# One inference step of a hybrid convolution / RWKV-7 decoder: block inversions as a stream of their own, and the last layer's MLP once per token group

## The chip, the cores and the metric

The kernel runs on one core of one Trainium2 chip. The metric is device time in microseconds (us) for one execution of the whole step; smaller is better. Three runs of the kernel before are shown, and one further execution was profiled.

## What is computed

The reference is a two-layer trunk over 1040 prompt tokens (16 learned meta tokens and 1024 prompt tokens) and 8 sampled tokens, model width 1024. Layer 0 mixes tokens with a Conformer convolution, layer 1 with RWKV-7; both are followed by a squared-ReLU MLP of width 4096. Cut to what matters here:

```python
def _wkv7_step(S, inp):
    r_t, w_t, k_t, v_t, kk_t, a_t = inp
    sa = jnp.einsum('bhvk,bhk->bhv', S, -kk_t)
    S = (S * w_t[:, :, None, :] + sa[..., None] * (kk_t * a_t)[:, :, None, :]
         + v_t[..., None] * k_t[:, :, None, :])
    y = jnp.einsum('bhvk,bhk->bhv', S, r_t)
    return S, y

def _sqrelu_mlp(h, w_in, w_out):
    return jnp.square(jax.nn.relu(h @ w_in)) @ w_out
...
    for i in range(DEPTH):
        ...
        h = h + out
        h = h + _sqrelu_mlp(_rmsnorm(h, norm_mlp[i]), w_mlp_in[i], w_mlp_out[i])
    return (_rmsnorm(h, norm_final), ...)
```

## The kernel before

**Arithmetic.** Everything is float32. A large product is made of three matmuls in a reduced-precision format: each operand is split into a high and a low part, and hi·hi, lo·hi and hi·lo are added in PSUM (`mm3`, lines 211 to 213). A weight tile of 128x1024 is loaded by SyncE (SP), its high part is made by ScalarE (ACT, line 177, `_hi`), and its low part by GpSimd (POOL) in four pieces, or by VectorE (DVE) in one (line 182, `_lo`). Raw tiles and split tiles go around in rings of a few buffers.

**Layer 0.** Convolution, then the MLP in three passes over the token groups `G0` of about 350 columns. In a pass, all 32 column tiles of `w_mlp_in` and 32 tiles of `w_mlp_out` are loaded and split once. Two passes have other work written beside them (the next group's convolution, above all DVE work). The third runs beside the first RWKV mixer group.

**Layer 1, mixers.** `mixer_in(g)` runs for four groups `G1` of 256 to 272 tokens: the projections k, r and v of eight tiles each (matmuls named `p_k`, `p_r`, `p_v`), low-rank parts, decays, and the operands of the recurrence, which go to DRAM. At the end of each tile, `finish` writes the 32x32 blocks `d_n` that are to be inverted.

**The recurrence** is done in 17 chunks: chunk 0 has the 16 meta tokens, chunks 1 to 16 have 64 tokens each. `front(c)` loads a chunk's operands and makes the products `A`; `chunk(c)` makes `gg`, `bT`, `W`, `po`, `U`, `S` and the output `Y` (lines 1284, 1311, 1351, 1359), each a short burst of small matmuls that waits for DVE or ACT to have moved the burst before. The state `sv` passes from chunk to chunk. Between chunks, `inverses(c, n)` inverts the blocks of chunk 0, and then of four chunks at a time (1 to 4, 5 to 8, ...), as 30 column steps of two DVE operations (lines 1243 and 1244), in SBUF. It is called inside `front(c)` for c = 0, 1, 5, 9 and 13, so it is part of the recurrence's one stream of work.

**What sets the order.** Each engine executes its own list in order. The lists come from the program's order and a scheduler's choice among what is ready. In the program, side work is a generator that gets `next()` at fixed places of the main work: `tick` gives the recurrence credit at each place of mixers 1 to 3 (`PACE`), and `filler(points, ...)` spreads several streams over the points of an MLP pass (`FA`, `NGA`, `NGB`, `FB` are the lengths it assumes).

**Layer 1, output and MLP.** Token groups `G2` have 328, 352 and 352 columns. After the mixers, `norm_gate` makes the gated output `z` of 128 tokens at a time from finished chunks, and `mixer_out(g)` multiplies by `rwkv_w_o` (`ps_oo`) and adds to the residual `h1`. Group 0 then has an MLP pass of its own, with the rest of the recurrence, the decode step of the 8 sampled tokens (`decode_step`, `ddec`, `Sdec`) and the gates of groups 1 and 2 beside it. Groups 1 and 2 have `mixer_out` one after the other, and then one common MLP pass in which each weight tile is used for both groups; `final(g)` (last norm, transposes `pf`, store) of groups 0 and 1 lie beside it.

**Buffers.** `new_act` makes an activation's high and low part as one tile each over all 8 row blocks (`[P, KT, n]`). `z` and the MLP's input `m1` of a group share one buffer.

## Time and profile before

| | us |
|---|---|
| median of 3 runs | 2793.69 |
| lowest and highest of them | 2791.5, 2795.14 |
| the profiled execution's own time | 2785.31 |
| its span from first to last instruction | 2783.6 |

| engine | busy us | share of the span |
|---|---|---|
| PE (matmul) | 2606.4 | 94% |
| DVE | 1994.5 | 72% |
| POOL | 1645.4 | 59% |
| ACT | 1355.2 | 49% |

The shares are averages over unlike stages, so they say little by themselves; the stages are cut apart in the rows below. TensorE's granted clock has two levels here, 2.4 GHz (1.0) and 1.2 GHz (0.5); the mean over the span was 0.973. A stretch with less than 1.0 ran in part at the lower level. DMA moved 428.32 MB, 154 GB/s on average.

### The profile page before, as it was taken

To read this page: it belongs to the slowest core of one execution; us is meant where nothing else is said; L and a number is where in the kernel's file an instruction comes from. 1 tells how busy PE (TensorE), PEld (TensorE's weight loads), DVE (VectorE), ACT (ScalarE), POOL (GpSimd) and SP (SyncE) were. 2 spreads that over 40 slices of the span, in tenths; PEclk is the share of its full clock that TensorE was granted. 3 is DMA by queue.
4 is the path that set the end of the run, shared out by engine and by line. 5 is a ranking of instruction groups with operands and counts; after the bars stand their busy time and mean duration, and the time that the engine had idled before them with its cause. 6 is when DMAs were issued, how large, how long until landed. Compare 5 with 4: busy or idle time off the path is not lost.

```text
span 2783.6 us, 54198 instructions
## 1 busy us (share of the span) xinstructions
PE 2606.4 (94%) x20554; PEld 2517.6 (90%) x20554; DVE 1994.5 (72%) x3752; ACT 1355.2 (49%) x2520; POOL 1645.4 (59%) x2191
## 2 busy tenths in 40 slices
PE   7998999999998999988789799979999999999998
PEld 7998999999998999978688688868889999999998
DVE  5999999996457454787897886877897654434445
ACT  5545444543355444565567757745434552222223
POOL 6686877887786354645443546647568773333332
PEclk9999999999999999998899899989999999999999
DMA  6563544454444555677788878876666632222211
GB/s 182 165 191 92 157 137 137 135 178 136 139 136 144 153 155 169 198 202 193 206 211 212 239 177 208 232 195 176 162 186 198 180 114 88 69 69 69 69 54 42
DMA packets 659284, 428.32 MB, mean 154 GB/s; under 512 B 126841, under 2 KB 609209, under 8 KB 659023
## 3 DMA queue, kind: packets, MB, share of 16 engines
q1 hardware_dynamic: 652780, 421.93, 54.0%
q8 instruction: 162, 2.65, 0.4%
q10 hardware_dynamic: 6018, 2.89, 0.4%
q14 instruction: 100, 0.81, 0.1%
q0 software_dynamic: 224, 0.03, 0.0%
HBM read 353.03 MB, written 72.66 MB: 153 GB/s over the span
## 4 chain that ended last, share of the span: by engine, by line
PE 59%; DVE 17%; POOL 8%; DMA 7%; issue 5%; ACT 4%; SPq 0%; DVEq 0%; ACTq 0%; POOLq 0%
PE ps_in L213 7%; PE ps_in L212 7%; PE ps_in L211 7%; PE out L212 7%; PE out L211 7%; PE out L213 7%; POOL wo_lo L182 4%; POOL wi_lo L182 3%; DVE cv L553 1%; DVE ni L1244 1%; DVE tt L1243 1%; DVE h L383 1%; PE ps_g L211 1%; PE ps_g L213 1%; PE ps_g L212 1%
## 5 line engine op out<-in xcount | busy, mean ns | idle before, releaser
L182 POOL TENSOR_TENSOR wo_lo<-wo_raw,wo_hi 128x256 fp32r<-128x256 f32 x672 | 521.8, 810 | 316.6 <-ACT wo_hi L177 294.2
L182 POOL TENSOR_TENSOR wi_lo<-wi_raw,wi_hi 128x256 fp32r<-128x256 f32 x600 | 464.7, 808 | 294.3 <-ACT wi_hi L177 284.4
L211 PE MATMUL out<-hh,wo_hi 128*128 128x352 f32 (+2 forms) x1536 | 498.9, 327 | 22.7 <-DVE h L383 10.5
L211 PE MATMUL ps_in<-m_h,wi_hi 128*128 128x352 f32 (+2 forms) x1536 | 498.0, 324 | 7.9 <-ACT m_h L304 6.2
L383 DVE TENSOR_TENSOR h<-h,out 128x352 f32<-128x352 f32 (+2 forms) x768 | 382.4, 508 | 167.3 <-PE out L213 166.6
L212 PE MATMUL out<-hh,wo_lo 128*128 128x352 f32 (+2 forms) x1536 | 496.2, 323 | 2.2 <-DVE wo_lo L182 2.2
L213 PE MATMUL ps_in<-m_l,wi_hi 128*128 128x352 f32 (+2 forms) x1536 | 495.1, 323 | 0.5 <-DVE m_l L305 0.5
L212 PE MATMUL ps_in<-m_h,wi_lo 128*128 128x352 f32 (+2 forms) x1536 | 494.1, 322 | 1.2 <-POOL wi_lo L182 1.2
L213 PE MATMUL out<-hl,wo_hi 128*128 128x352 f32 (+2 forms) x1536 | 491.5, 322 | 1.6 <-DVE hl L160 1.6
L553 DVE SCALAR_TENSOR_TENSOR cv<-u,wdw,cv 128x352 f32<-128x352 f32 (+2 forms) x720 | 376.5, 572 | 0.7
L177 ACT CAST wi_hi<-wi_raw 128x1024 fp32r<-128x1024 f32 x160 | 167.9, 1049 | 375.8 <-PE out L213 193.5
L177 ACT CAST wo_hi<-wo_raw 128x1024 fp32r<-128x1024 f32 x184 | 192.6, 1048 | 311.6 <-PE ps_in L213 152.7
L211 PEld LDWEIGHTS out<-hh,wo_hi 128*128 128x128 f32 x1536 | 289.7, 189 | 31.5 <-DVE h L383 13.6
L211 PEld LDWEIGHTS ps_in<-m_h,wi_hi 128*128 128x128 f32 x1536 | 290.0, 189 | 11.3 <-ACT m_h L304 6.4
L212 PEld LDWEIGHTS out<-hh,wo_lo 128*128 128x128 f32 x1536 | 291.2, 190 | 4.2 <-DVE wo_lo L182 2.9
L212 PEld LDWEIGHTS ps_in<-m_h,wi_lo 128*128 128x128 f32 x1536 | 289.8, 189 | 3.2 <-POOL wi_lo L182 2.0
L213 PEld LDWEIGHTS out<-hl,wo_hi 128*128 128x128 f32 x1536 | 289.8, 189 | 2.4 <-DVE hl L160 2.1
L213 PEld LDWEIGHTS ps_in<-m_l,wi_hi 128*128 128x128 f32 x1536 | 289.0, 188 | 2.0 <-DVE m_l L305 0.9
L370 DVE SCALAR_TENSOR_TENSOR r<-ps_in,rs_m 128x352 f32<-128x352 f32 (+2 forms) x192 | 98.3, 514 | 219.0 <-PE ps_in L213 215.4
L160 DVE TENSOR_TENSOR hl<-s,hh 128x352 fp32r<-128x352 f32 (+2 forms) x192 | 135.9, 709 | 100.6 <-ACT hh L159 100.3
L372 ACT ACTIVATE s<-r 128x352 f32<-128x352 f32 (+2 forms) x192 | 93.6, 490 | 141.6 <-DVE r L370 139.4
L182 POOL TENSOR_TENSOR wv_lo<-wv_raw,wv_hi 128x256 fp32r<-128x256 f32 x96 | 83.4, 900 | 32.0 <-ACT wv_hi L177 18.0
(409 smaller groups left out, 6122.9 us busy)
## 6 DMA issues: line engine op xcount, KB each, us to landing
wi_raw<-in_w_mlp_in_dram SPq DMA_DIRECT2D x160, 512.0 KB
wo_raw<-in_w_mlp_out_dram SPq DMA_DIRECT2D x160, 512.0 KB
wk_raw<-in_rwkv_w_k_dram SPq DMA_DIRECT2D x32, 512.0 KB
wr_raw<-in_rwkv_w_r_dram SPq DMA_DIRECT2D x32, 512.0 KB
wv_raw<-in_rwkv_w_v_dram SPq DMA_DIRECT2D x32, 512.0 KB
d_ab<-ab SPq DMA_DIRECT2D x32, 512.0 KB
pg_raw<-in_conv_w_pw_dram SPq DMA_DIRECT2D x24, 512.0 KB
pa_raw<-in_conv_w_pw_dram SPq DMA_DIRECT2D x24, 512.0 KB
```

The lines of the kernel that those rows point to most:

```text
L160: eng_lo.tensor_sub(lo, src, hi.bitcast(F32))
L177: nc.scalar.copy(hi[:, :a * b], raw[:, :a * b])
L182: eng_lo.tensor_sub(lo[:, cs], raw[:, cs], hi[:, cs].bitcast(F32))
L211: nc.tensor.matmul(ps, w[0], act[0], start=first, stop=False)
L212: nc.tensor.matmul(ps, w[1], act[0], start=False, stop=False)
L213: nc.tensor.matmul(ps, w[0], act[1], start=False, stop=last)
L370: nc.vector.scalar_tensor_tensor(r[:, :n], ps[:, :n], 0.0, rs[:, :n], op0=ALU.max, op1=ALU.mult)
L372: nc.scalar.activation(s[:, :n], r[:, :n], AF.Square)
L383: nc.vector.tensor_add(hv[:, 4 * i + m, :], hv[:, 4 * i + m, :], ps[:, :n])
L553: nc.vector.scalar_tensor_tensor(acc[m][:, :n], ug[:, m, j:j + n], wdw[:, m, j:j + 1], acc[m][:, :n], op0=ALU.mult, op1=ALU.add)
L1243: nc.vector.tensor_mul(o, ni[:, :j, j:j + 1].broadcast_to([B, j, wd]), ni[:, j:j + 1, j + 1:].broadcast_to([B, j, wd]))
L1244: nc.vector.tensor_add(ni[:, :j, j + 1:], ni[:, :j, j + 1:], o)
```

## The change

It has four parts.

1. **Inversions.** `inverses` is no longer called from `front`. A generator `inversions` goes through all blocks in order, and is advanced by its own credit (`invert`) at the ticks of the mixers, in the loop behind them, and once per step of the recurrence in the MLP passes. A chunk now waits for `st["inv"]` in place of `st["ready"]`. The inversion of chunk 0 covers the 16 meta tokens alone (14 column steps in place of 30).
2. **Pace.** The recurrence gets `PACE` 1.3 per tick in mixers 1 to 3 (before 1.7, 1.7 and 0.98), without the inversions in it.
3. **Three passes.** The common MLP pass of groups 1 and 2 is gone: each group has `mixer_out` and then an MLP pass of its own, so the weights of layer 1's MLP are loaded and split three times, not twice. The recurrence is cut at the chunks that each group's gates need: up to 11 beside pass 0, up to 16 beside pass 1. The decode step stands ahead of the gates. The ring of raw tiles has 4 buffers in these passes (before 5), that of split tiles 4 (before 5).
4. **Activation tiles.** `new_act` makes one tile per row block, 8 for each part.

The diff, cut to its core:

```diff
         def new_act(pl, name, nmax, tag="act"):
-            return (pl.tile([P, KT, nmax], F32R, name=f"{name}_h", tag=f"{tag}h"),
-                    pl.tile([P, KT, nmax], F32R, name=f"{name}_l", tag=f"{tag}l"))
+            return tuple([pl.tile([P, nmax], F32R, name=f"{name}_{q}{k}", tag=f"{tag}{q}", bufs=KT) for k in range(KT)] for q in "hl")
...
-            for b in range((last - lag) // 2, nj // 2 - 1):
-                yield from outs(b)
-            w, wo = load_in(last), list(load_out(nj // 2 - 1))
+            if layer == 0:
+                for b in range((last - lag) // 2, nj // 2 - 1):
+                    yield from outs(b)
+            w = load_in(last)
             for group in groups:
                 yield from inp(last, w, group)
-                for i in range(2):
-                    yield from out(nj // 2 - 1, i, wo[i], group)
-                if done and group is not groups[-1]:
-                    done(group[0])
+            for b in range(nj // 2 - 1 if layer == 0 else (last - lag) // 2, nj // 2):
+                yield from outs(b)
...
-            B = n * 32
+            B, W = n * 32, 32 if c else META
...
-            for j in range(30, 0, -1):
-                wd = 31 - j
+            for j in range(W - 2, 0, -1):
+                wd = W - 1 - j
...
-                if j % 4 == 0:
-                    yield 1.5
+                yield 1
...
+        def inversions():
+            for c, n in [(0, 1)] + CHUNKS:
+                while st["ready"] < c + n - 1:
+                    yield None
+                yield from inverses(c, n)
+                st["inv"] = c + n - 1
+        inv = inversions()
...
-            if c == 0:
-                yield from inverses(0, 1)
-            if c % 4 == 1:
-                yield from inverses(c, 4)
...
-            while c > st["ready"]:
+            while c > st["inv"]:
                 yield None
...
-        PACE = [0, 1.7, 1.7, 0.98]
+        PACE = [0, 1.3, 1.3, 1.3]
+        INV_PACE, INV_SLOW = 1.0, 0.3
...
+            invert(INV_PACE * (slow if slow == 1 else INV_SLOW))
             advance(PACE[g] * slow, NCH - 1)
...
-            raw_f, wsp_f = raw_pool(l1, "f", 3), split_pool(l1, "f", 2)
+            raw_f, wsp_f = raw_pool(l1, "f", 2), split_pool(l1, "f", 1)
...
             def until(last):
                 while st["done"] < last:
+                    invert(1.0)
                     with tc.high_priority(offset=RE):
                         wait = next(rec)
-                    yield wait
+                    yield 1 if wait is None else wait
...
+            def whole(g, actp, *streams):
+                fill, rest = filler(2 * KT + MLP_POINTS, *streams)
+                add, sums = sums_of(g)
+                mixer_out(g, actp, fill, add)
                 n = G2[g][1]
                 hv = hl[g][:, :, :n]
-                return (g, hv, n, *mlp_in(actp, hv, n, 1, f"m1{g}", sums), hidp)
...
+                mlp(1, [(g, hv, n, *mlp_in(actp, hv, n, 1, f"m1{g}", sums), hidp)], 2, MW1, nc.vector, fill)
+                for _ in rest:
+                    pass
...
+            whole(0, actp, ([until(last[1])], FA * chunk_waits(last[1])), ([decode_step(), norm_gates(GN_OF[1])], NGA))
+            whole(1, actp, ([ranked(FN, final(0))], FB), ([until(last[2])], FA * chunk_waits(last[2])), ([norm_gates(GN_OF[2])], NGB))
...
-            mixer_out(1, residp2, actp, fill, add)
...
-            mixer_out(2, residp2, actp2, fill, add)
...
-            mlp(1, [g1, group(2, actp2, hidp2, sums)], 1, nc.gpsimd, nc.vector, fill2, done)
...
+            whole(2, actp2, ([ranked(FN, final(1))], FB))
+            for _ in final(2):
+                pass
```

How the lists of the engines move, at three places. First VectorE, where chunk 0's inversion begins, in mixer 1 (`tt0_j` and `ni0` are its column steps, `wk1_5_lo` is a split of a weight of mixer 1's k projection, `bv0_7` the last operation of mixer 0). Before:

```order
L1137 TENSOR_TENSOR bv0_7_14533<-vv0_7_14273,pk0_7_14531 128x272
L1243 TENSOR_TENSOR tt0_30_14575<-ni0_14541 32x30
L1244 TENSOR_TENSOR ni0_14541<-ni0_14541,tt0_30_14575 32x30
L1243 TENSOR_TENSOR tt0_29_14578<-ni0_14541 32x58
L1244 TENSOR_TENSOR ni0_14541<-ni0_14541,tt0_29_14578 32x29x2
L1243 TENSOR_TENSOR tt0_28_14581<-ni0_14541 32x84
```

Now:

```order
L1136 TENSOR_TENSOR bv0_7_14659<-vv0_7_14399,pk0_7_14657 128x272
L1241 TENSOR_TENSOR tt0_14_14749<-ni0_14667 32x14
L1242 TENSOR_TENSOR ni0_14667<-ni0_14667,tt0_14_14749 32x14
L1241 TENSOR_TENSOR tt0_13_14764<-ni0_14667 32x26
L1242 TENSOR_TENSOR ni0_14667<-ni0_14667,tt0_13_14764 32x13x2
L1241 TENSOR_TENSOR tt0_12_14787<-ni0_14667 32x36
```

It begins at the same place, and has 28 operations of at most 56 elements per partition where it had 60 of up to 240.

Second TensorE, at the end of the mixers (`nn3_7`, `pk3_7` are mixer 3's last tile, a name with a chunk's number such as `W11` belongs to the recurrence, `ps_oo0` is `mixer_out` of group 0). Before:

```order
L1135 MATMUL pk3_7_22574<-rk3_7_22536,hsum_10012 128x264
L1351 MATMUL bT110_23064<-ident_58,bk11_22471 128x128 x4
L1351 MATMUL bT111_23070<-ident_58,bk11_22471 128x128 x4
L1359 MATMUL W11_23161<-sv_14395,xa1_14402 64x64 x16
L1311 MATMUL po11_23162<-p3211_22477,gg11_22921 32x32 x16
L1284 MATMUL A120_23202<-xa0_14399,bk12_23080 128x256 x2
L1284 MATMUL A122_23210<-xa0_14399,bk12_23080 128x256 x2
L1517 MATMUL yn3_1_23233<-ident_58,ey3_1_23013 128x128 x4
L1359 MATMUL U11_23283<-w111_23195,p6411_23056 64x64 x16
L1284 MATMUL A124_23358<-xa0_14399,bk12_23080 128x256 x2
L1359 MATMUL S11_23416<-uv_14396,bkt11_23063 64x64 x16
L211 MATMUL ps_oo0_0_22670<-z0_h_22627,wo0_0_hi_22663 128x328
```

Now:

```order
L1134 MATMUL pk3_7_22410<-rk3_7_22372,hsum_10138 128x264
L1285 MATMUL A100_22908<-xa0_14525,bk10_22668 128x256 x2
L1285 MATMUL A102_22916<-xa0_14525,bk10_22668 128x256
L1360 MATMUL U9_23189<-w19_22901,p649_22644 64x64 x16
L1285 MATMUL A102_22916<-xa0_14525,bk10_22668 128x256
L1285 MATMUL A104_23237<-xa0_14525,bk10_22668 128x256 x2
L211 MATMUL ps_oo0_0_22523<-z0_h0_22466,wo0_0_hi_22516 128x328
```

The recurrence is two chunks less far when the last layer's output product begins. Counted over the lists, TensorE meets 1, 5 and 6 bursts `W` in mixers 1, 2 and 3 before, and 2, 3 and 5 now; the other 7 of the 17 come after `ps_oo0` begins, 3 of them beside pass 0 and 4 beside pass 1 (before 5, all beside pass 0).

Third TensorE, where group 1's output product ends (`st_m11` is the sum for its norm, `ps_in1_0_1` the first product of its MLP). Before:

```order
L213 MATMUL ps_oo1_7_27972<-z1_l_27665,wo1_7_hi_27965 128x352
L266 MATMUL st_m11_28008<-acc_m110_27809,ones_d_63 128x352
L266 MATMUL st_m11_28008<-acc_m111_27848,ones_d_63 128x352
L211 MATMUL ps_oo2_0_28080<-z2_h_28037,wo2_0_hi_28073 128x352
L212 MATMUL ps_oo2_0_28080<-z2_h_28037,wo2_0_lo_28074 128x352
L266 MATMUL st_m11_28008<-sq1_6_27961,ones_d_63 128x352
```

Now:

```order
L213 MATMUL ps_oo1_7_26968<-z1_l7_26572,wo1_7_hi_26961 128x352
L265 MATMUL st_m11_27022<-acc_m110_26761,ones_d_63 128x352
L265 MATMUL st_m11_27022<-acc_m111_26800,ones_d_63 128x352
L1657 MATMUL pf000_27521<-ident_58,h1_0_22464 128x128 x2
L211 MATMUL ps_in1_0_1_27074<-m11_h0_27031,wi1_1_0_hi_27065 128x352
L212 MATMUL ps_in1_0_1_27074<-m11_h0_27031,wi1_1_0_lo_27066 128x352
```

Before, the next group's output product stood between; now the MLP's first product follows with two transposes in between, and needs the row block `m11_h0` that ScalarE makes from the product just ended. The same holds for group 2.

## Rows read from the trace of the kernel before

**Rows 1.** The page, part 1: the span, and each engine's busy time.

```profile
span 2783.6 us, 54198 instructions
PE 2606.4 (94%) x20554; PEld 2517.6 (90%) x20554; DVE 1994.5 (72%) x3752; ACT 1355.2 (49%) x2520; POOL 1645.4 (59%) x2191
```

**Rows 2.** Busy time by stage: mixers 1, 2, 3, output, passes, end.

```profile
core 0: us, PE busy (x) PEld busy (x) DVE busy (x) ACT busy (x) POOL busy (x), PEclk, DMA share, GB/s
1240.20:1411.70 171.50, 136.60 (x1270) 125.91 (x1270) 146.76 (x285) 98.49 (x219) 80.63 (x103) 0.86 0.76 201
1411.70:1610.50 198.80, 172.73 (x2235) 156.70 (x2233) 164.95 (x306) 138.41 (x311) 90.69 (x113) 0.94 0.84 219
1610.50:1833.00 222.50, 192.14 (x2647) 174.88 (x2645) 167.98 (x331) 149.63 (x364) 123.95 (x185) 0.95 0.83 212
1833.00:1881.20 48.20, 38.98 (x396) 37.04 (x396) 42.79 (x86) 20.78 (x40) 24.90 (x31) 0.93 0.60 154
1881.20:2201.80 320.60, 300.79 (x2709) 284.96 (x2710) 253.11 (x503) 155.52 (x289) 223.64 (x273) 0.99 0.64 180
2201.80:2267.50 65.70, 65.10 (x399) 63.63 (x397) 39.24 (x51) 36.65 (x62) 56.48 (x71) 1.00 0.53 153
2267.50:2770.00 502.50, 502.37 (x3149) 501.16 (x3148) 221.03 (x412) 139.43 (x225) 184.91 (x246) 1.00 0.21 65
2770.00:2783.60 13.60, 4.42 (x39) 3.86 (x37) 5.74 (x11) 5.48 (x12) 0.94 (x1) 0.72 0.40 135
```

**Rows 3.** The same view, the start of mixer 1 alone.

```profile
1240.20:1264.00 23.80, 14.44 (x95) 12.39 (x96) 16.99 (x31) 8.47 (x25) 15.85 (x24) 0.58 0.64 180
```

**Rows 4.** The same view, line 1243 alone (busy: DVE), chunk 0's inversion.

```profile
1260.00:1322.00 62.00, 14.07 (x30) 0.91 0.75 184
```

**Rows 5.** DVE's timeline (start us, duration us, operation), near that inversion's end.

```profile
1318.49 0.21 DVE L1243 TENSOR_TENSOR tt<-ni 32x58 f32<-32x58 f32 x1
```

**Rows 6.** The same view as rows 2 by source line: A, then W U S Y.

```profile
1240.20:1833.00 592.80, 57.51 (x208) 37.18 (x208) 0.92 0.81 211
1240.20:1833.00 592.80, 64.62 (x1792) 58.14 (x1792) 0.92 0.81 211
```

**Rows 7.** The same view and stretch: bT, then gg and po.

```profile
1240.20:1833.00 592.80, 14.20 (x96) 10.52 (x96) 0.92 0.81 211
1240.20:1833.00 592.80, 17.20 (x768) 14.31 (x768) 0.92 0.81 211
```

**Rows 8.** Groups of DVE, 1234 to 1833 us: what empties A.

```profile
L1291 DVE TENSOR_TENSOR xa<-A,m_ar 64x128 f32<-64x128 f32 x101 | 28.9, 288 | 17.5 <-ACT no L1290 15.2
...
L1292 DVE TENSOR_TENSOR nr<-A,m_ar 128x256 f32<-128x256 f32 x50 | 20.3, 406 | 0.0
```

**Rows 9.** Waits of PE, 1234 to 1445 us: us in total, times, longest.

```profile
PE nn L1117 <- DVE ab L1200: 9.9, 1, 9.9
PE p_k L213 <- DVE ml L160: 6.2, 1, 6.2
```

**Rows 10.** PE's timeline at the end of the mixers.

```profile
1822.89 3.75 PE L1284 MATMUL A<-xa,bk 128*128 128x256 f32 x8 [10.68 <-DMA bk<-d_ab]
```

**Rows 11.** Waits of PE, 1833 to 2060 us, and the clock just behind the longest.

```profile
PE ps_in L211 <- ACT m_h L304: 6.2, 1, 6.2
...
1881.20:1888.00 6.80, 5.85 (x19) 5.02 (x20) 6.80 (x12) 5.99 (x13) 6.22 (x9) 0.50 0.53 157
```

**Rows 12.** Busy time by stretch: layer 0's second and first MLP pass.

```profile
600.00:800.00 200.00, 198.94 (x1250) 197.99 (x1250) 124.04 (x235) 82.23 (x115) 158.40 (x211) 1.00 0.49 149
300.00:520.00 220.00, 219.27 (x1370) 217.75 (x1370) 213.52 (x441) 98.06 (x149) 172.73 (x237) 1.00 0.47 140
```

**Rows 13.** The page, part 5: GpSimd's splits of MLP weights, over the whole span.

```profile
L182 POOL TENSOR_TENSOR wo_lo<-wo_raw,wo_hi 128x256 fp32r<-128x256 f32 x672 | 521.8, 810 | 316.6 <-ACT wo_hi L177 294.2
L182 POOL TENSOR_TENSOR wi_lo<-wi_raw,wi_hi 128x256 fp32r<-128x256 f32 x600 | 464.7, 808 | 294.3 <-ACT wi_hi L177 284.4
```

**Rows 14.** Waits of POOL, 1833 to 2203 us, beside pass 0.

```profile
POOL sw L1369 <- DVE sv L1411: 25.3, 4, 13.6
```

More of the change, by code (lines that the diff above doesn't have):

```diff
@@ L339, in hybrid_step, with mlp, mlp_steps @@
         HR = 0
-        def mlp(layer, groups, lag, eng_w, eng_h, fill=None, done=None):
-            for _ in mlp_steps(layer, groups, lag, eng_w, eng_h, done):
+        def mlp(layer, groups, lag, eng_w, eng_h, fill=None):
+            for _ in mlp_steps(layer, groups, lag, eng_w, eng_h):
                 if fill:
                     fill()
-        def mlp_steps(layer, groups, lag, eng_w, eng_h, done=None):
+        def mlp_steps(layer, groups, lag, eng_w, eng_h):
             w_in, w_out = w_mlp_in[layer], w_mlp_out[layer]
@@ L1300, in step @@
         def step(c):
-            if c < NCH and c <= st["ready"]:
+            if c < NCH and c <= st["inv"]:
                 if c not in fronts:
@@ L1447, in advance, with invert @@
             st["credit"] = min(st["credit"], 0)
+        def invert(wait):
+            st["inv credit"] += wait
+            while st["inv credit"] > 0:
+                w = next(inv, None)
+                if w is None:
+                    break
+                st["inv credit"] -= w
+            st["inv credit"] = min(st["inv credit"], 0)
         def decode_step():
@@ L1575, in hybrid_step @@
         carry["tail"]()
-        advance(CHUNK_WAIT * NCH, NEED[GN_OF[0][-1]])
+        while st["done"] < NEED[GN_OF[0][-1]]:
+            invert(2)
+            advance(2, NEED[GN_OF[0][-1]])
         for _ in ng0:
@@ L1655, in until, with chunk_waits @@
                 while st["done"] < last:
+                    invert(1.0)
                     with tc.high_priority(offset=RE):
                         wait = next(rec)
-                    yield wait
+                    yield 1 if wait is None else wait
+            def chunk_waits(last):
+                return sum(CHUNK_WAIT for c in range(st["done"] + 1, last + 1))
             def sums_of(g):
                 n = G2[g][1]
-                return square_sums(n, f"m1{g}", lambda k: cur["tmp"].tile([P, cur["n"]], F32, name=f"sq{g}_{k}", tag="sq", bufs=3)[:, :n],
-                                   (nc.gpsimd, nc.vector))
@@ L1665, in group @@
[L1665 removed]
+                return square_sums(n, f"m1{g}", lambda k: tt(f"sq{g}_{k}", "t2")[:, :n], (nc.gpsimd, nc.vector))
+            def whole(g, actp, *streams):
+                fill, rest = filler(2 * KT + MLP_POINTS, *streams)
+                add, sums = sums_of(g)
+                mixer_out(g, actp, fill, add)
                 n = G2[g][1]
                 hv = hl[g][:, :, :n]
[L1668 removed]
@@ L1671, in hybrid_step @@
-            ng2 = norm_gates(GN_OF[2])
-            fill, rest = filler(2 * KT + MLP_POINTS,
-                                ([until(NCH - 1)], FA * CHUNK_WAIT * (NCH - 1 - st["done"])),
-                                ([norm_gates(GN_OF[1]), decode_step(), ng2], NGA))
-            add, sums = sums_of(0)
-            mixer_out(0, residp, actp, fill, add)
-            mlp(1, [group(0, actp, hidp, sums)], 2, nc.gpsimd, nc.vector, fill)
-            for _ in rest:
-                pass
-            lw.close()
@@ L1681, in hybrid_step @@
-            outp = pool(l1, "outp", 1)
-            cur["wide"] = max(n for lo, n in G2[1:])
-            residp2, actp2, hidp2 = pool(l1, "resid2", 2, **right), pool(l1, "actp2", 1, **right), pool(l1, "hidp2", 2, **right)
-            fill, rest = filler(2 * KT, ([ng2], NGB))
-            add, sums = sums_of(1)
-            mixer_out(1, residp2, actp, fill, add)
-            for _ in rest:
-                pass
+                mlp(1, [(g, hv, n, *mlp_in(actp, hv, n, 1, f"m1{g}", sums), hidp)], 2, MW1, nc.vector, fill)
@@ L1689, in hybrid_step @@
+                for _ in rest:
+                    pass
+            MW1 = nc.gpsimd
+            last = [NEED[gs[-1]] for gs in GN_OF]
+            whole(0, actp, ([until(last[1])], FA * chunk_waits(last[1])), ([decode_step(), norm_gates(GN_OF[1])], NGA))
+            whole(1, actp, ([ranked(FN, final(0))], FB), ([until(last[2])], FA * chunk_waits(last[2])), ([norm_gates(GN_OF[2])], NGB))
+            lw.close()
+            actp2 = pool(l1, "actp2", 1, **right)
             for q in range(DEC):
@@ L1690, in hybrid_step @@
                 nc.scalar.dma_start(o_conv_sample[0, q, 0:CB - 1, :], state_conv[0, q, 1:CB, :])
-            g1 = group(1, actp, hidp, sums)
-            fill, rest = filler(2 * KT + MLP2_POINTS, ([ranked(FN, final(0))], FB))
-            add, sums = sums_of(2)
-            mixer_out(2, residp2, actp2, fill, add)
-            end = []
-            def done(g):
-                end.append(filler(KT, ([final(g)], 24)))
-            def fill2():
-                (end[0][0] if end else fill)()
-            mlp(1, [g1, group(2, actp2, hidp2, sums)], 1, nc.gpsimd, nc.vector, fill2, done)
@@ L1703, in hybrid_step @@
-            for it in (rest, end[0][1], final(2)):
-                for _ in it:
-                    pass
+            whole(2, actp2, ([ranked(FN, final(1))], FB))
+            for _ in final(2):
+                pass
 _INS = ['x_prompt', 'x_sample', 'state_conv', 'state_shift', 'state_wkv', 'meta_tokens',
```

30 lines of the change are left out of this document (15 added, 15 removed).

## The prediction

> **What bounds the kernel now.** I read the page first, then the busy time by stage, then the waits and the timeline of the stages that lose time. The page has TensorE (PE) busy for 2606.4 of 2783.6 us [rows 1], so at most 177 us of idle time are to be had, plus what the lower clock costs. The stage view shows where they are [rows 2]. As a measure of work I take PE's busy time times the granted clock of the stage. Mixer 1 has 136.60 x 0.86 = 117 us of it in 171.5 us, so 54 are lost; mixer 2 has 162 in 198.8 (36 lost); mixer 3 has 183 in 222.5 (40 lost). The output product of group 0 loses 12 of 48, pass 0 loses 23 of 320.6, and the stretch from 2201.8 to 2770 us loses less than 1 of 568. Some 130 us are thus lost in the three mixers, 35 behind them, and none in the common pass of groups 1 and 2, which this change takes apart. Up to mixer 1 the lists of all engines are alike but for a few swaps, so all before about 1266 us stays as it is.
>
> Mixer 1 is near the limit of VectorE (DVE): 146.76 of 171.5 us busy [rows 2], and PE's longest waits there are for DVE [rows 9]. Mixer 2 is at 83% on DVE, mixer 3 at 75%.
>
> **Chunk 0's inversion.** Its 30 first operations take 14.07 us [rows 4], and there are as many second ones, so about 28 us of DVE. What is left are 28 operations of at most 56 elements; one of 58 takes 0.21 us [rows 5], so some 5.6 us. DVE in mixer 1 loses 22 us of work. It also gets one chunk more. Its TensorE cost is the next thing to price.
>
> **A chunk, and where it goes.** A: 57.51 us for 208 records, 16 per chunk, is 4.4 us. W, U, S, Y: 64.62/1792 x 160 = 5.8 us [rows 6]. bT: 14.20/12 = 1.2, gg and po: 17.20/12 = 1.4 [rows 7]. Together 12.8 us at a mean clock of 0.92, 12 us of work. On DVE, emptying A takes 8 x 0.288 + 4 x 0.406 = 3.9 us [rows 8]; with as much again for the copies and the state I take 8, an estimate. Counting all these bursts in the lists, mixer 1 gains one chunk (+12), mixers 2 and 3 lose about one and a half each (-18, -18), and 24 us go behind the mixers.
>
> - Mixer 1: DVE 146.8 - 22 + 8 = 133; with the 25 us that it idled, 158. PE's work is 129, and 23.8 - 14.44 x 0.58 = 15 are lost in the first 24 us [rows 3], before anything changes. I take 162: **-9**.
> - Mixer 2: 18 less work, and 36 were lost beside 5 chunks. If a chunk causes only a part of them, 3 us are saved with the chunks gone: **-21**.
> - Mixer 3: the same 18; of its 40 lost, 10.68 is one wait for the load of a chunk's `bk` at the very end [rows 10]. The new list has the same product A, waiting for a load, at the same place, so I leave that wait. 3 for the chunks: **-21**.
>
> Bounds of the lost time that the mixers give back: none (the stalls belong to their own weights and mixes), and 60 of the 130 (chunks and inversions cause all but the start and the end).
>
> **Behind the mixers.** The moved work: **+24**. What a chunk costs beyond its work is read in pass 0: of 23 lost, 6.2 are the wait for `m_h` and 3.4 the slow clock behind it (6.8 us at 0.50) [rows 11], which leaves 13 for 5 chunks, 2.6 each. Two more: **+5**.
>
> The wait at the start of an MLP pass: 6.2 us, since the MLP's input shares its buffer with `z` and is one tile, free only when the last product is through. With one tile per row block, the first is free one column of products earlier, 24 matmuls or 3.8 us (502.37 us for 3149 matmuls [rows 2]), so I take 3 to 4 us for a start. Group 0 gains 5, groups 1 and 2, whose starts lay beside each other's work, pay 4 each: **+3**. Bounds: 9.6 gained (no wait at any start), and 2 x 9.6 paid (each like the old one). The Trainium skill (TensorE: Matmul & The Clock Gate, "HAM oscillation") says that an array left waiting falls to the lower clock and begins the next group on it, so that a wait costs more than its length. The trace agrees at group 0's start. By that rule every start would cost like the old one, and the sum would be 16 higher.
>
> **The third reading of the weights.** 64 weight tiles more are loaded, cast and split. On POOL that is 256 x 0.81 us = 207 us [rows 13] beside a pass of 502.4/2 = 251 us of PE. Layer 0 has this very pattern: its second pass is on PE for 198.94 of 200 us with POOL at 158 and DMA at 149 GB/s, and its first pass for 219.27 of 220 us though DVE is busy for 213.52 [rows 12]. I cost it at **0**, and the cover is POOL's idle sixth and the ring ahead: 4 split tiles of 24 matmuls, some 15 us (19 with 5). If the cover fails, see the second rival. The smaller raw ring, the other places of the decode step and of the final norms go with it. ACT and SP have room (ACT 155 of 320 us in pass 0 [rows 2]). In the last pass, the outputs of the last two blocks follow the last input product, so the chain of the last hidden block lies beside 48 matmuls; the end of 13.6 us stays. Small risks there and in the list of loads: **+2**.
>
> **The sum.** Mixers -9 - 21 - 21 = -51. Behind them 24 + 5 + 3 + 2 = +34. Together -17, from the 2785.31 us of the profiled execution to 2768. That execution is 8.4 us (0.3%) below the median shown, 2793.69, so against the median I say 2777.
>
> **The rivals.**
> 1. *The work moves and the stalls stay* (slower). Mixer 1 to 3 wait for DVE's weight splits, mixes and `ab`, which all remain, so they give back the moved work and a little of chunk 0's inversion, 30 us. Behind them 24 + 5 and starts at nearly the old price, 16, come to +45. Together +15: 2809. It decides from the point where the mixers take over 559 us in all. For it: mixer 1 lost 54 us with a single chunk in it. Against it: most of that chunk's company on DVE was inversion.
> 2. *GpSimd holds up the weights.* In pass 0, POOL waits for the state `sv` before `sw` for 25.3 us in 4 waits, up to 13.6 [rows 14], and the splits behind it in its list wait too. With a ring shorter by a tile, 3 us for each of 7 chunks would reach PE: -17 + 21 = +4, 2798. Against it: PE shows no such wait in pass 0.
> 3. *Every start costs like group 0's.* If each pass begins with a wait of 6.2 us and 6.8 us at the lower level [rows 11], two more cost 2 x 9.6 = 19 in place of 3: -1, 2793. For it: the chain from the last product to the first row block (add, activation) is the same. Against it: the row blocks come free one by one. It is the case that the Trainium skill's clock rule, named above, would expect.
> 4. *The mixers were held by the inversions.* As part of the chain they stop it in front of chunks 1, 5 and 9, and DVE's splits behind them. Spread out and ahead, 55 of the 130 lost us return, where the forecast has 51 - 24 = 27: mixers -79, behind them +34, together -45: 2749. For it: mixer 1, with two inversions in it, lost most. Against it: mixers 2 and 3, with one each, lose only 18% of their time, and DVE has the same work in them.
>
> **How the numbers follow.** My forecast has 0.45 (2762 to 2792), rival 1 0.20, rival 2 0.08, rival 3 0.12, rival 4 0.15. A measurement of this kernel tells 0.2%, 5.6 us, from no change. Faster: 0.42 of the forecast's and rival 4: 0.57. The same: 0.03 of the forecast's, 0.10 of rival 3 and 0.02 of rival 2: 0.15. Slower: rival 1 and the rest of rivals 2 and 3: 0.28. The range of 8 in 10 goes from 2746, a little past rival 4, to 2808, the near half of rival 1.
>
> **What would show it.** In the profile after: no DVE operation of chunk 0's inversion over 0.3 us; mixers 1 to 3 together near 542 us (over 559: rival 1); the stretch from the first `ps_oo` to the end near 985 us. PE's wait for `m_h` or `m11_h0` at three starts of 3 to 4 us each and a clock of 1.0 behind them (rival 3 if it is 0.5); PE at 99% in the third pass with no waits for `wi_lo` or `wo_lo` (rival 2 if there are). I am wrong if the mixers' DVE share falls while they take as long: then PE waited for something that I have not read.

## The result, and the profile after

The change makes the kernel **slower**: 2823.89 us (median of 4 runs, 2819.91 to 2825.70) beside 2792.84 us for the kernel before, a ratio of 1.0105 (95% interval 1.0093 to 1.0118). I had said 2777, with a range of 2746 to 2808. The profiled execution took 2819.91 us.

The page's first part for the changed kernel, which answers to [rows 1]:

```profile
span 2817.9 us, 54952 instructions
PE 2655.4 (94%) x20554; PEld 2540.7 (90%) x20554; DVE 1988.2 (71%) x3720; ACT 1416.4 (50%) x2580; POOL 1833.5 (65%) x2447
```

The span grew by 34.3 us, and PE's busy time by 49.0, with the same 20554 matmul records. So PE does not wait longer; the same matmuls keep it busy longer. Every row of a stage, here and below, is from one profiled execution, and one execution can lie some us off its kernel's median: that of the kernel before lies 7.5 us below, this one 4.0 below. The stage view says where (columns as in [rows 2]; the stages are mixers 1, 2 and 3, output product of group 0, pass 0, output of group 1, pass 1, output of group 2, pass 2, end):

```profile
1242.60:1421.20 178.60, 152.12 (x1549) 136.06 (x1549) 144.73 (x284) 108.08 (x245) 84.92 (x112) 0.91 0.84 212
1421.20:1602.80 181.60, 158.50 (x1846) 145.21 (x1840) 138.64 (x254) 117.52 (x262) 78.20 (x96) 0.92 0.75 203
1602.80:1815.00 212.20, 178.22 (x2221) 161.16 (x2221) 154.19 (x295) 135.03 (x330) 114.54 (x183) 0.93 0.81 206
1815.00:1865.80 50.80, 46.32 (x455) 42.41 (x453) 42.60 (x104) 22.07 (x47) 21.34 (x28) 0.93 0.67 175
1865.80:2175.60 309.80, 293.03 (x2121) 269.40 (x2117) 230.36 (x433) 134.22 (x225) 223.52 (x274) 0.96 0.57 162
2175.60:2213.30 37.70, 37.70 (x224) 34.38 (x223) 13.65 (x19) 19.67 (x33) 30.39 (x38) 1.00 0.54 140
2213.30:2521.60 308.30, 307.99 (x2627) 295.44 (x2626) 174.68 (x330) 147.15 (x262) 204.62 (x264) 1.00 0.55 155
2521.60:2553.80 32.20, 32.20 (x200) 31.73 (x199) 15.98 (x21) 18.16 (x30) 31.02 (x40) 1.00 0.48 140
2553.80:2804.00 250.20, 250.20 (x1571) 249.62 (x1570) 115.22 (x206) 98.11 (x138) 183.85 (x246) 1.00 0.43 128
```

Mixers 1 to 3 take 572.4 us where they took 592.8: 20 less, and I had said 51 less. From the first `ps_oo` to the end it is 1003 us where it was 950.6: 52 more, and I had said 34 more. With 2 more ahead of mixer 1 that is the whole difference.

The last line is the third reading of the weights with nothing of the recurrence beside it: PE is busy for 250.20 of 250.20 us. So what is too long lies ahead of it, in a stretch with chunks beside the products. PE's timeline in pass 0, beside chunk 11 (start us, duration us, then the instruction; `out` are the MLP's second products, `po` one of a chunk's bursts of 32 small records):

```profile
1928.65 0.31 PE L211 MATMUL out<-hh,wo_hi 128*128 128x328 f32 x1
1928.80 0.31 PE L212 MATMUL out<-hh,wo_lo 128*128 128x328 f32 x1
...
1930.44 0.42 PE L211 MATMUL out<-hh,wo_hi 128*128 128x328 f32 x1
1930.79 0.24 PE L1312 MATMUL po<-p,gg 32*32 32x32 f32 x2
1930.96 0.41 PE L212 MATMUL out<-hh,wo_lo 128*128 128x328 f32 x1
1931.31 0.24 PE L1312 MATMUL po<-p,gg 32*32 32x32 f32 x2
...
1933.40 0.31 PE L1312 MATMUL po<-p,gg 32*32 32x32 f32 x2
1933.64 0.64 PE L211 MATMUL out<-hh,wo_hi 128*128 128x328 f32 x1
1934.22 0.31 PE L1312 MATMUL po<-p,gg 32*32 32x32 f32 x2
```

A burst that PE should run in one piece is **cut**: two records of `po`, one product of the MLP, two records, one product. Two products in a row start 0.15 us apart (1928.65, 1928.80). A product with a piece of `po` takes 0.52 us (1930.44 to 1930.96), and 0.82 a little later (1933.40 to 1934.22), at half the clock. PE's list of instructions has the same pattern, here beside chunk 12 (one instruction of `po` is two records of the trace; the names end in buffer numbers):

```
11586 L213 MATMUL out_13_0_1_26244<-hl_26_25991,wo_0_13_0_hi 128x328
11587 L1312 MATMUL po_26806<-p_24358,gg_24914 32x32
11588 L211 MATMUL out_13_0_1_26244<-hh_26_25990,wo_0_13_0_hi 128x328
11589 L1312 MATMUL po_26806<-p_24358,gg_24914 32x32
11590 L212 MATMUL out_13_0_1_26244<-hh_26_25990,wo_0_13_0_lo 128x328
```

So the order was fixed before the program ran. In the list before, no burst stands in more than two pieces. In the changed list 17 bursts stand in three or more, 125 pieces in all: 36 pieces of 5 bursts in the mixers (chunks 1 to 3), 89 pieces of 12 bursts that the program writes behind them (chunks 9 to 12 and 16).

The bursts are written inside `burst(lead, rest)`, lines 833 to 843, under `tc.high_priority(offset=BURST)` with `BURST = 400`: the scheduler ranks them as if they had been written 400 instructions earlier. The change does not touch these lines. It changes when a chunk becomes ready, and so what else is ready beside it. That the scheduler alternates because a burst's rank then falls among the ranks of ready products is my reading of this line; the scheduler itself was not looked into. What follows tests what the cuts cost.

### The profile page after: what moved, and what is told of

It is laid out like the page before. It is cut to its first block, busy times and chain, and to the rows that moved or that the text cites. A ratio compares the mean times of both kernels' runs of the same rounds, so it can differ in the third digit from the quotient of the medians.

```text
span 2817.9 us, 54952 instructions
## 1 busy us (share of the span) xinstructions
PE 2655.4 (94%) x20554; PEld 2540.7 (90%) x20554; DVE 1988.2 (71%) x3720; ACT 1416.4 (50%) x2580; POOL 1833.5 (65%) x2447
## 4 chain that ended last, share of the span: by engine, by line
PE 65%; DVE 14%; DMA 7%; POOL 6%; issue 4%; ACT 3%; SPq 1%; ACTq 0%; DVEq 0%; POOLq 0%
PE out L211 7%; PE out L212 7%; PE out L213 7%; PE ps_in L211 7%; PE ps_in L212 7%; PE ps_in L213 7%; POOL wi_lo L182 2%; POOL wo_lo L182 2%; DVE cv L552 1%; PE ps_oo L211 1%; PE ps_oo L212 1%; PE A L1285 1%; PE ps_oo L213 1%; PE ps_g L211 1%; PE Y L1360 1%
## 5 line engine op out<-in xcount | busy, mean ns | idle before, releaser
L182 POOL TENSOR_TENSOR wo_lo<-wo_raw,wo_hi 128x256 fp32r<-128x256 f32 x800 | 606.6, 790 | 263.2 <-ACT wo_hi L177 224.5
L182 POOL TENSOR_TENSOR wi_lo<-wi_raw,wi_hi 128x256 fp32r<-128x256 f32 x728 | 574.1, 820 | 212.5 <-ACT wi_hi L177 206.7
L211 PE MATMUL out<-hh,wo_hi 128*128 128x352 f32 (+2 forms) x1536 | 506.8, 333 | 22.7 <-DVE h L383 8.3
L383 DVE TENSOR_TENSOR h<-h,out 128x352 f32<-128x352 f32 (+2 forms) x768 | 383.0, 509 | 168.3 <-PE out L213 167.0
L177 ACT CAST wo_hi<-wo_raw 128x1024 fp32r<-128x1024 f32 x216 | 226.3, 1050 | 345.8 <-PE out L213 152.9
L177 ACT CAST wi_hi<-wi_raw 128x1024 fp32r<-128x1024 f32 x192 | 201.4, 1049 | 355.3 <-PE ps_in L213 165.5
L211 PEld LDWEIGHTS out<-hh,wo_hi 128*128 128x128 f32 x1536 | 291.7, 191 | 33.4 <-DVE h L383 10.3
L160 DVE TENSOR_TENSOR hl<-s,hh 128x352 fp32r<-128x352 f32 (+2 forms) x192 | 147.1, 768 | 79.8 <-ACT hh L159 79.6
```

Source lines behind the costliest of these rows:

```text
L160: eng_lo.tensor_sub(lo, src, hi.bitcast(F32))
L177: nc.scalar.copy(hi[:, :a * b], raw[:, :a * b])
L182: eng_lo.tensor_sub(lo[:, cs], raw[:, cs], hi[:, cs].bitcast(F32))
L211: nc.tensor.matmul(ps, w[0], act[0], start=first, stop=False)
L383: nc.vector.tensor_add(hv[:, 4 * i + m, :], hv[:, 4 * i + m, :], ps[:, :n])
```

## The experiments

The kernel before, run again beside the experiments, took 2791.95 or 2791.96 us (medians) beside experiments 1 to 8 and 2795.99 beside experiments 9 to 11. Each ratio is to the kernel before that ran beside it.

**1. Whole bursts.** The changed kernel with one number changed:

```diff
-        BURST = 400
+        BURST = 4000
```

> The changed kernel with BURST 4000 in place of 400, so that the scheduler places a burst of the recurrence ahead of all waiting MLP products. In the changed kernel's TensorE list 17 bursts are cut into 3 to 18 pieces with MLP or projection products in between (po12 into 15, Y12 into 18); here two are cut, into 3 pieces. Theory A (cut bursts cost TensorE time, and the clock falls in them): pass 0 goes from 310 us to about 292, no stretch at 1.2 GHz inside it, and the whole is 15 to 25 us shorter than the changed kernel, near 2802 as a median. Theory B (the moved chunks cost what they cost, cut or whole, and the stalls of the mixers stay): within 5 us of the changed kernel, 2819 to 2829.

Measured: 2785.51 us, ratio 0.9977 (0.9967 to 0.9987). This kernel is 38.4 us below the changed kernel's 2823.89 (the kernels before that ran beside the two are 0.9 us apart). That is theory A's direction, and more than its 15 to 25. In its list 2 bursts with 6 pieces are left. The page:

```profile
span 2786.8 us, 54937 instructions
PE 2615.5 (94%) x20554; PEld 2524.9 (91%) x20554; DVE 1985.3 (71%) x3720; ACT 1414.9 (51%) x2580; POOL 1827.9 (66%) x2447
```

PE's busy time is 39.9 us less than in the changed kernel, and the span of the profiled execution 31.1: the whole gain is there, none in waits. By stage (mixers 1, 2 and 3, output product of group 0, pass 0, output of group 1, pass 1):

```profile
1244.10:1432.50 188.40, 155.99 (x1670) 142.56 (x1670) 144.53 (x291) 111.30 (x254) 84.14 (x114) 0.89 0.82 204
1432.50:1609.30 176.80, 153.00 (x1799) 141.16 (x1797) 143.78 (x259) 117.49 (x266) 76.93 (x97) 0.91 0.78 211
1609.30:1812.10 202.80, 175.86 (x2281) 160.28 (x2281) 149.41 (x294) 132.64 (x324) 108.61 (x179) 0.95 0.79 208
1812.10:1868.40 56.30, 45.86 (x484) 43.12 (x484) 46.26 (x99) 25.61 (x53) 29.89 (x37) 0.94 0.75 197
1868.40:2150.40 282.00, 263.03 (x1978) 253.96 (x1977) 223.90 (x423) 130.55 (x215) 215.10 (x266) 0.98 0.61 173
2150.40:2182.50 32.10, 32.10 (x198) 31.63 (x198) 14.63 (x21) 17.94 (x30) 30.17 (x39) 1.00 0.46 134
2182.50:2490.60 308.10, 307.82 (x2626) 295.26 (x2625) 174.41 (x331) 147.39 (x262) 204.52 (x264) 1.00 0.54 155
```

Pass 0 and the output of group 1 behind it, where chunks 11 and 12 were cut, are 33.4 us shorter (282.0 and 32.1, from 309.8 and 37.7); the output of group 0 is 5.5 longer. Pass 1, with four chunks and only one burst in three pieces, takes 308 us in both kernels: nothing was too long there. A whole burst in PE's timeline, beside the same kind of product:

```profile
1874.91 0.31 PE L211 MATMUL ps_in<-m_h,wi_hi 128*128 128x328 f32 x1
1875.15 0.69 PE L1312 MATMUL po<-p,gg 32*32 32x32 f32 x32
1875.77 1.46 PE L265 MATMUL st_m<-sq,ones_d 128*128 128x328 f32 x2
```

All 32 records take 0.69 us, so two are 0.04. A product and two records should then take 0.19 us; cut, they take 0.52. Each cut thus costs some 0.33 us at the full clock, and more at the lower one. From 125 pieces of 17 bursts (108 cuts) to 6 of 2 (4 cuts) there are 104 cuts fewer, 0.37 us each if they make the 38.4 us. The two figures agree, since a part of the cuts ran at the lower clock.

The groups by line of passes 0 and 1 show it as well: the same 192 records of `po`, first in the changed kernel, then here (behind the bar: busy us, mean ns):

```profile
L1312 PE MATMUL po<-p,gg 32*32 32x32 f32 x192 | 10.5, 203 | 0.0
```

```profile
L1312 PE MATMUL po<-p,gg 32*32 32x32 f32 x192 | 4.2, 192 | 0.0
```

**2. Whole bursts behind the mixers only.** The same number, set after the mixers' buffers are closed:

```diff
         ld.close()
+        BURST = 4000
```

> The same edit, but BURST is 4000 only behind the mixers; the cut bursts of chunks 1 and 2 in mixers 1 and 2 stay as in the changed kernel. Theory A: 12 to 18 us shorter than the changed kernel, all of it in pass 0 and the output product behind it, mixers at 572 us as before; the run with the edit everywhere is a few us shorter still. Theory B: within 5 us of the changed kernel.

Measured: 2793.99 us, ratio 1.0003 (0.9994 to 1.0012), in theory A's direction, and once more beyond its 12 to 18. So 29.9 of the 38.4 us were lost in the passes, 8.5 in the mixers. By cuts it is 73 and 31; at 0.35 us, 26 and 11.

**3. The number alone.** The kernel before with `BURST = 4000`: a control, since no burst is cut there with either number.

> Control: the kernel before with BURST 4000. None of its bursts is cut at 400 or at 4000. Theory A (it was the cuts that cost): nothing to gain, 2787 to 2797. Rival B (a burst ahead of everything is worth as much to any kernel, whatever was cut): 2755 to 2775.

Measured: 2800.50 us, ratio 1.0033 (1.0024 to 1.0043). Rival B is refuted. The number itself gains nothing and costs 0.33%, which theory A had not either: its mixers take 605.3 us in place of 592.8, behind them it is 950.0 as before. So experiment 1 gained because the cuts went, and in spite of this.

**4 and 5. Either half of the change**, with `BURST = 400`. Both have the activation tiles of the change. The stream alone has the new mixers and the passes of before:

```diff
-        PACE = [0, 1.7, 1.7, 0.98]
+        PACE = [0, 1.3, 1.3, 1.3]
+        INV_PACE, INV_SLOW = 1.0, 0.3
...
-            if c == 0:
-                yield from inverses(0, 1)
-            if c % 4 == 1:
-                yield from inverses(c, 4)
```

> The changed kernel's mixers (inversion stream, short inversion of chunk 0, pace 1.3, one tile per row block) with the passes behind the mixers as before (groups 1 and 2 in one pass, all remaining chunks beside pass 0). Mixers about 572 us, as in the changed kernel, 20 less than before. Theory A: the stretch behind them is that of before, 951 us, and one more chunk at 12 to 15 us, so the whole is 5 to 8 us shorter than before, near 2786. Theory B: a chunk costs the same wherever it lies, so the 20 us of the mixers come back whole behind them, and the whole is within 5 us of before, 2788 to 2798.

Measured: 2803.73 us, ratio 1.0035 (1.0024 to 1.0047), over both expectations. Its mixers take 593.7 us, not 572, with 11 chunks in them where the changed kernel has 10, and the stretch behind them 964.8. The passes alone have the mixers of before and:

```diff
+            whole(0, actp, ([until(last[1])], FA * chunk_waits(last[1])), ([decode_step(), norm_gates(GN_OF[1])], NGA))
+            whole(1, actp, ([ranked(FN, final(0))], FB), ([until(last[2])], FA * chunk_waits(last[2])), ([norm_gates(GN_OF[2])], NGB))
...
+            whole(2, actp2, ([ranked(FN, final(1))], FB))
```

> The mixers as before (inversions inside the recurrence, pace 1.7, 1.7, 0.98) with the three passes of the change. Mixers about 593 us. In its TensorE list chunk 12's bursts are cut as in the changed kernel (po12 into 16 pieces, U12 into 9), chunk 10's a little. Theory A: behind the mixers 980 to 990 us, 30 to 40 more than before, half of it in cut bursts; whole near 2828. Theory B: the three passes cost only their starts and a cut or not makes no difference, 951 plus 5 to 12; whole near 2802.

Measured: 2816.66 us, ratio 1.0091 (1.0071 to 1.0111), nearer to theory A's 2828 than to B's 2802. Its mixers take 589.6 us and the stretch behind them 989.7. Either half alone makes the kernel slower, and either has cut bursts: 6 bursts in 39 pieces, and 9 in 53.

**6 and 7. Either half with whole bursts**, the same two kernels with `BURST = 4000`.

> The stream of inversions alone, with whole bursts (BURST 4000; the passes as before). Theory A: 8 to 15 us shorter than the same kernel with cut bursts (2803.7), as the edit was worth 8 us in the mixers of the changed kernel. Theory C (the mixers are held by chains of their own, not by chunks or inversions): mixers 565 to 575 and behind them 955 to 965, so 2783 to 2793, no measurable gain on before or just one. Theory D (inversions held the mixers): mixers 540, whole near 2765.

> The three passes alone, with whole bursts (mixers as before, inversions inside the recurrence). Theory A: the 25 us that this part cost were cut bursts for the most part; now mixers 590, behind them 955 to 965, whole 2790 to 2802. If the third reading of the weights or the three starts cost in themselves: 2810 or more.

Measured: 2791.46 us, ratio 1.0002 (0.9992 to 1.0013), and 2793.25 us, ratio 1.0009 (0.9996 to 1.0022), both as theory A has it for the whole. (The stream's mixers still take 586.6 us, so theory D is refuted, and theory C's 565 to 575 missed.) The cuts cost the stream 12.3 us for 31 cuts fewer, and the passes 23.4 for 40. The second is more than the 14 that 0.35 us a cut makes; what the rest is stays open. The four runs of the passes with cut bursts lie up to 14 us apart.

With whole bursts there are now four kernels: 2800.50 with neither half, 2791.46 with the stream, 2793.25 with the passes, 2785.51 with both. The last three also have the activation tiles, the first has not. So the stream and the tiles are worth 9.0 us, the passes and the tiles 7.3, all three 15.0. The tiles alone gained 0.15%, some 4 us (experiment 9, with `BURST = 400`); if they are worth as much here, the halves are worth 5 and 3, and all three come to 12 where 15.0 was measured. The 15.0 lie near the 17 that I had forecast, but against a base that is 8.5 us slower than the kernel before. Against the kernel before, experiment 1 gains 6.4.

**8. Fewer chunks in the mixers.** Experiment 1 with the recurrence's pace at zero:

```diff
-        PACE = [0, 1.3, 1.3, 1.3]
+        PACE = [0, 0, 0, 0]
```

> The changed kernel with whole bursts and pace 0 in the mixers: the recurrence gets no credit there, and the scheduler pulls chunks 0 to 6 into the mixers from behind; 7 bursts W lie in the mixers in place of 10, so about 3 chunks more beside the passes. Theory C: a chunk costs the mixers its own work and no more, 11 to 13 us, so mixers 530 to 540, behind them 1010 to 1020, and the whole within 6 us of the run with pace 1.3 (2785.5). Theory D: a chunk in the mixers costs 18 us or more (work and stalls), so mixers below 515 and the whole 10 to 20 us shorter than with pace 1.3.

Measured: 2826.56 us, ratio 1.0130 (1.0109 to 1.0150), outside of both expectations. The mixers take 577.6 us with 7 chunks, where experiment 1 takes 568.0 with 10. The stage view, mixers 1 to 3, and PE's longest wait in mixer 3 (us in total, times, longest):

```profile
1243.47:1414.44 170.97, 142.42 (x1412) 128.66 (x1412) 139.75 (x268) 101.44 (x230) 82.30 (x110) 0.89 0.81 211
1414.44:1568.96 154.52, 141.01 (x1591) 130.87 (x1587) 126.50 (x232) 104.74 (x232) 77.65 (x96) 0.96 0.80 222
1568.96:1821.10 252.14, 165.16 (x1998) 150.39 (x1996) 169.77 (x342) 131.73 (x319) 109.83 (x175) 0.83 0.70 189
```

```profile
PE yn L1528 <- DVE ey L1524: 52.5, 4, 17.7
```

Mixers 1 and 2 are short, but at the end of mixer 3 the gates of group 0 are late, and PE stands still for them. The run gives a rough price of a chunk. Counted by `W`, mixer 2 has 2 chunks here and 5 before, and 126.50 us of DVE in place of 164.95, with the same number of inversion steps. That is 12.8 us of DVE for each chunk, and 14.8 us of time (154.52 against 198.80). Counted by all records of the bursts the difference is 2.5 chunks, which makes it 15 and 17.

**9 to 11. Row tiles alone, and two other paces.** First the kernel before with nothing but the activation tiles of the change:

```diff
-            return (pl.tile([P, KT, nmax], F32R, name=f"{name}_h", tag=f"{tag}h"),
+            return tuple([pl.tile([P, nmax], F32R, name=f"{name}_{q}{k}", tag=f"{tag}{q}", bufs=KT) for k in range(KT)] for q in "hl")
```

> Edit: the kernel before, with its MLP activations and its z split into one tile per row block, as in the change; schedule, passes and bursts as before. Theory of the prediction (a start of a pass costs what its first row block is late): the wait for m_h at pass 0 goes from 6.2 us to 4 or less, and the half-clock stretch behind it shortens or goes; stretch behind the mixers 950.6 to about 945; time 2786 to 2789, ratio 0.998 to 0.999. Rival (the wait is moved to the next thing that is late): the wait is there under another name, time within 2 us of the kernel before.

Measured: 2790.66 us, ratio 0.9985 (0.9970 to 0.9999). The wait for `m_h` is gone, but PE's waits from 1870 to 1900 us show it under other names, in all 6.1 us:

```profile
PE ps_in L213 <- DVE m_l L304: 3.7, 2, 3.0
PE ps_in L211 <- DVE h L1604: 2.4, 1, 2.4
```

So the rival is right on the wait: the first product starts earlier, and the next ones wait for the low parts and for the residual. The granted clock is 0.64 from 1881 to 1888 us and 0.63 in the 7 us behind, so the stretch at the lower level is there too. The wait now lies behind the first product of pass 0, so by stage it counts as pass 0: that is 7.2 us longer (327.8 from 320.6), the output product 9.7 shorter (38.5 from 48.2), and the stretch behind the mixers 949.4, not 945. What makes the 0.15% of time is not settled; the interval all but reaches 1.

Then experiment 1 with fewer chunks beside the early mixers, but not none:

```diff
-        PACE = [0, 1.3, 1.3, 1.3]
+        PACE = [0, 0.6, 0.6, 2.0]
```

> Edit: the change with whole bursts, and the pace of the chunks [0, 0.6, 0.6, 2.0] in place of [0, 1.3, 1.3, 1.3]: fewer chunks beside mixers 1 and 2, more beside mixer 3. Theory A (a chunk beside mixer 2 costs about 15 us for 12 of work, and a chunk beside mixer 3 or a pass 12 to 13): 2 to 3 chunks moved save 5 to 8 us, time 2778 to 2782. Theory B (what counts is the number of chunks that group 0's gates need by the end of mixer 3, wherever they lie, and a later start only makes the end serial, as with pace 0): time 2788 or more, with PE waiting at the end of mixer 3 for what the gates need.

Measured: 2775.31 us, ratio **0.9936** (0.9918 to 0.9954), the fastest of all, below both kernels. Theory B is refuted. Theory A has the direction, but one chunk moved where it had 2 to 3, and 10 us were saved where it had 5 to 8. And with `[0, 1.3, 0.9, 2.0]`:

> Edit: the change with whole bursts, and the pace of the chunks [0, 1.3, 0.9, 2.0]: mixer 1 as in the whole-burst version, one chunk or so moved from mixer 2 to mixer 3. Theory A: one chunk by 3 us, time 2782 to 2785. Theory B: within 2 us of the whole-burst version (2785.5) or over it, with the same end of mixer 3.

Measured: 2786.04 us, ratio 0.9970 (0.9955 to 0.9985), which tells neither theory from the other: by the ratio it is 2784 us against the base of experiment 1. The stage view of the fastest, mixers 1 to 3:

```profile
1241.30:1424.70 183.40, 154.92 (x1660) 140.83 (x1660) 147.38 (x292) 111.86 (x259) 90.27 (x119) 0.89 0.85 214
1424.70:1590.60 165.90, 146.69 (x1734) 136.53 (x1731) 138.50 (x254) 113.50 (x253) 72.69 (x93) 0.94 0.79 215
1590.60:1795.20 204.60, 170.43 (x2214) 155.54 (x2214) 154.43 (x291) 135.53 (x326) 116.54 (x177) 0.95 0.82 215
```

The mixers of three kernels with whole bursts, us and chunks, counted by the records of `W`:

| kernel | mixer 1 | mixer 2 | mixer 3 | sum | behind |
|---|---|---|---|---|---|
| experiment 1 | 188.4, 3 | 176.8, 3 | 202.8, 4 | 568.0, 10 | 974.7 |
| pace 0.6, 0.6, 2.0 | 183.4, 3 | 165.9, 2 | 204.6, 5 | 553.9, 10 | 977.1 |
| pace 1.3, 0.9, 2.0 | 182.8, 3 | 168.3, 2 | 216.9, 6 | 567.9, 11 | 974.9 |

One chunk moved from mixer 2 to mixer 3 gained 11 in the one and cost 2 in the other; one chunk more in mixer 3 cost 12 and gained 2 behind. Why mixer 3 took the first for so little isn't settled: each of these is one profiled execution, and the paces also move the chunks' places within a mixer.

## Why the prediction was wrong, and where it was right

**The step that failed** is the cost of the recurrence beside the MLP passes: "The moved work: **+24**", and "13 for 5 chunks, 2.6 each. Two more: **+5**". It takes a chunk's price from pass 0 of the kernel before, where no burst stands in more than two pieces. There was no term for bursts cut among products, which cost 38 us (experiments 1 and 2: 30 behind the mixers, 8.5 in them). Without them the stretch behind the mixers is 974.7 us (experiment 1), 24 more than before, where I had 34 more; with them 52 more. The direction turned on this: with whole bursts the change is 6.4 us faster than the kernel before, with cut ones 31 slower. It was in reach: the lists of both kernels showed the pattern before any run, and I had counted whole bursts in them, not pieces.

Without the cuts the forecast would still have been 10 us too good, and that it is no more is luck: by the two profiled executions the mixers gave back 26 us less than I had said, and the stretch behind them cost 10 less.

No rival named the cuts. Rival 1 lies nearest in time (2809), and its deciding point was passed: the mixers took 572 us, over 559. Its half on the mixers holds: it had 30 us given back, and they gave 20, or 25 with whole bursts. Its half behind them does not: it had +45, with starts at nearly the old price, and with whole bursts it is +24.

**The second miss: the mixers**, -51 forecast, -20 measured, -25 with whole bursts. By mixer I had 162, 178 and 201; it came to 178.6, 181.6 and 212.2 [rows 2 for before]. By the forecast's own measure (busy time times granted clock), the mixers lost 130 us before, and I had 27 of them return; they lose some 122 in the changed kernel and as many in experiment 1. So about 8 return: most stalls stayed when chunks and inversions moved. Two terms were mis-sized:
- A chunk on DVE is 12.8 us or more (experiment 8), where I took 8 as an estimate from the operations that empty A. The inversions in mixer 1 saved 18.9 us, not 22: chunk 0's and that of chunks 1 to 4 had 55.4 us (lines 1243 and 1244), and now have 36.5. With these, mixer 1 with two chunks should have 146.8 - 18.9 + 12.8 = 140.7 us of DVE; experiment 8 has 139.75, the changed kernel 144.73.
- "With the 25 us that it idled" took DVE as the limit of mixer 1. With two whole-burst chunks it takes 171.0 us (experiment 8): DVE idles for 31 of them. The time that DVE gave free did not come back on PE.

The sentence with which I had said that I would be wrong came true in good part: DVE's share over the three mixers fell from 81% (479.7 of 592.8 us) to 76% (437.6 of 572.4), and the time fell by 3%. What PE waited for in place of DVE is only seen in part. PE's longest sum of waits in the three mixers of the changed kernel is four waits for a chunk's load `bk`, 14.9 us, and such waits are there before as well [rows 10 for the longest]. Rival 4, that the inversions held the mixers up (-79), did not come: in the stream they are spread, and the mixers return a third of that at most in the changed kernel and experiment 1, and half (38.9) in the fastest.

**Chunk 0's inversion**: "no DVE operation of chunk 0's inversion over 0.3 us" was wrong for four of its 28, and its sum is 7.29 us, not 5.6; the section on the hardware shows them.

**Right.** The third reading of the weights costs PE nothing: 250.20 of 250.20 us at a clock of 1.00, and no wait of PE for `wi_lo` or `wo_lo` from the first `ps_oo` to the end (rival 2 refuted). POOL pays for it: it is busy for 1833.5 us in place of 1645.4, the 188 that I had put at 207.

**Right for groups 1 and 2, and too dear:** the starts of the passes. In the changed kernel none of the three waits for `m_h` or `m11_h0`, and the longest wait at one is 0.4 us, for `m_l`; I had 3 to 4 us each, and the old start has 6.2 [rows 11]. The starts of groups 1 and 2 have no wait in experiment 1 either, so rival 3 is refuted for the two starts that it priced. Group 0's start is another matter: with whole bursts it waits 3.4 us for `m_l` (experiment 1), and beside the old schedule 6.1 (experiment 9). Row tiles do not remove that wait by themselves.

**The Trainium skill's clock rule** (TensorE: Matmul & The Clock Gate, "HAM oscillation") would have had each start cost more than its wait. The changed kernel's starts don't test it, as none waited. Group 0's start does in two experiments, and both agree: behind the 3.4 us of experiment 1 the granted clock was 0.50 from 1875.8 to 1879.2 us, and experiment 9 is told above.

## What to carry to other kernels

When a change moves small urgent work beside a long stream of products, look in the order of the instructions for bursts that are split up, and price every cut: here 0.33 us, twice the product between. It appeared as busy time of PE with the same number of matmul records, not as a wait, so the view of waits didn't show it. A schedule is tuned with its numbers: `BURST = 400` was right for the old order and cost 38 us in the new one, and the pace of the chunks, tried again after that, was worth another 0.4%.
